# First projections of a two-layer trunk: plain fp32r products against seven block products in scaled fp16 parts

## The chip, the cores and the metric

The kernel runs on one core of a Trainium2 chip. The metric is the device time of one launch, in microseconds (us). The kernel before takes 2886.77 us, the median of three runs (2885.02 to 2900.39).

## The reference, cut to what matters

Two post-norm layers, `x <- LayerNorm(alpha * x + mixer(x))`, over 2048 tokens of 1024 features. Layer 0 is forgetting attention with 8 heads of 128, layer 1 sparse attention over keys chosen by an indexer. The change lies in the first statement of layer 0:

```python
def _fox_mixer(x, w_in, b_f, w_out):
    ...
    q, k, v, f_logit, gate = _split(x @ w_in, [H * dh, H * dh, H * dh, H, D])
    ...
    log_f = jax.nn.log_sigmoid((f_logit + b_f).astype(jnp.float32))
    cum = jnp.cumsum(log_f, axis=1)
    ...
    s = jnp.einsum('bqhd,bshd->bhqs', q_b, k).astype(jnp.float32) * scale
    s = s + jnp.transpose(c_b, (0, 2, 1))[..., None] - cum_t[:, :, None, :]
    ...
    return (jax.nn.silu(gate) * o.reshape(B, S, D)) @ w_out
```

`x @ w_in` is a product of 2048 x 1024 by 1024 x 4104: queries, keys and values of 1024 columns each, 8 columns of forget logits, and 1024 columns of gate.

## The kernel before, in words

The stages follow each other: the first projections (`fox_proj`), forgetting attention (`attention(0)`), its output projection with the projections and the index of layer 1, attention of layer 1, its output projection. TensorE goes through them without a break between stages.

**Precision.** A product of fp32 operands is made of three matmuls (`mm3`, lines 308 to 313): high part by high part (L310), high by low (L311), low by high (L312). In `fox_proj` the parts are of type fp32r. `split` (L318 to L320) makes them: ACT copies the high part (L319), and GpSimd (POOL) or, for tokens, VectorE (DVE) subtracts it for the low part (`sub`, L316).

**Tiles.** A query, key or gate tile is 128 columns of `w_in` (numbers 0 to 7 queries, 8 to 15 keys, 16 to 23 gates) by all tokens, in four chunks of 512 tokens. `weights` (L323) reads a tile as two pieces of 128 x 512 and splits each; `proj` (L331) makes 8 x 3 matmuls of 512 columns for a chunk into one bank of PSUM, weights stationary. That is 24 x 4 x 24 = 2304 matmuls. Values are turned: the tokens are stationary, the columns of the values move, in slices of 384, 384 and 264 columns (`VW`; the last has the 8 forget logits). `values` makes 16 x 24 matmuls for each slice: 768 of 384 columns, 384 of 264.

**Evacuation.** Gate tiles go through ACT (`to_dram`, L345). Queries, keys and values are scaled and cut into two fp16 parts for attention: ACT makes the high part (L352), DVE the rest (L353), and SP stores both.

**Scales and the scan.** The fp16 parts need scales, powers of two taken from the largest magnitudes of the tokens and of every weight tile. `bounds` (L455 to L532) is the scan: it reads the weights once more, 512 KB at a time through the two QS buffers (L477), DVE reduces each to a column of maxima (L470), `find` gathers them (L494), TensorE turns the columns (L496), DVE reduces across (L498), `spread` brings the results to all partitions with a small matmul (L502) and works out the scales (L503 to L523).

**Order.** The chunks of the first three gate tiles come first, while the tokens are loaded and split. The scan runs beside gate tiles 19 to 21, five reads a chunk (`SCAN`); `find` stands between the halves of tile 23. Then come the values' last slice, tile 0, the forget gates (`fox_gates`), and the rest. The order within an engine is set when the program is built: its scheduler places rows by the dependencies and by its own idea of time. SP issues all reads and stores in one order.

Of the kernel before, what the change touches and what calls it, by code (L numbers as in the profile page):

```python
# [41 lines left out]
VW = (384, 384, 264)  # L42
# [6 lines left out]
         {"K": 4, "V": 2, "PT": 1, "PU": 1, "PX": 1, "PR": 4, "PP": 3, "M": 1, "N": 3}, {"P": 8})  # L49
ORDER = ((), ("N", "I", "PR", "PT", "pad1", "PU", "K", "PP", "V", "PX"),  # L50
         ("N", "M", "PX", "PT", "PU", "pad2", "PR", "K", "V", "PP"), ("pad3", "P"))
SIZE = {"K": 2048, "V": 4096, "PT": 8192, "PU": 8192, "PX": 8192, "PR": 4096, "PP": 4096, "I": 128, "N": 256,
        "M": 2432, "pad1": 3200, "pad2": 896, "pad3": 4096, "P": 4096}
# [18 lines left out]
SCAN = 5  # L72
FINDS = (0, 1), (2, 3)
# [59 lines left out]
def lay_out(inp):  # L133
# [10 lines left out]
    o["fw"] = mtiles(np.concatenate([fw[:, 0:2048], fw[:, 3080:4104]], 1))  # L144
    for i, n in enumerate(VW):
        v = fw[:, 2048 + 384 * i:2048 + 384 * i + n].reshape(2, 4, 128, n)
        o["fv%d" % i] = c(v.transpose(0, 2, 1, 3).reshape(2, 128, 4 * n))
# [26 lines left out]
def trunk(tc, A, out, taps=None):  # L174
    nc = tc.nc
    with ExitStack() as ctx:
        K = Trunk(ctx, tc, A, out)
        with K.phase(0):
            K.fox_proj()
# [42 lines left out]
class Trunk:  # L222
    def __init__(self, ctx, tc, A, out):
# [28 lines left out]
        self.flog = self.sb.tile([128, NT, 8], F32, name="flog")  # L252
        self.wi = self.flog
# [4 lines left out]
    def constants(self):  # L258
        nc, A = self.nc, self.A
        mf = self.e([128, 128])  # L260
        nc.sync.dma_start(self.ident, A["ident"])
        nc.sync.dma_start(self.kvg, A["kvg"])
        nc.sync.dma_start(mf, A["cmask"])
        nc.sync.dma_start(self.zt, A["ztab"].rearrange("p (a b) -> p a b", a=4))
        nc.vector.tensor_copy(self.cmask, mf)
# [93 lines left out]
    def to_planes(self, name, row, scale):  # L359
        def evac(ps, ch):  # L360
            t, parts = self.pair()
            self.planes(parts, ps, scale)
            to = self.scr[name]
            to = to[ch, row:row + 128] if name == "q1" else to[row:row + 128, :, ch * 512:(ch + 1) * 512]
            self.nc.sync.dma_start(to, t)
        return evac

    def fox_proj(self):
        nc, A = self.nc, self.A
        X = {}  # L370
        xv = A["xT"].rearrange("(g k p) t -> g p k t", k=4, p=128)
        first = (16, 17, 18)
        W = {}
        for ch in range(NCH):
            for g in range(2):
                hi, lo = self.t("KV", [128, 4, 512], R), self.t("P", [128, 4, 512], R)
                for k in range(4):
                    if ch == 0 and (g, k) in ((0, 0), (0, 2), (1, 0)):
                        m = first[len(W)]
                        W[m] = self.weights(A["fw"][m])  # L380
                    raw = self.e([128, 512])
                    nc.sync.dma_start(raw, xv[g][:, k, ch * 512:(ch + 1) * 512])
                    self.split(hi[:, k], lo[:, k], raw, nc.vector)
                X[g, ch] = hi, lo
        self.constants()

        def tile(m, chunks=range(NCH)):
            row = m % 8 * 128
            evac = (self.to_planes("q1", row, self.scale("cq", 0)), self.to_planes("k1", row, self.scale("k", 0)),
                    self.to_dram("g1", row, AF.Silu))  # L390
            self.proj(W.get(m) or self.weights(A["fw"][m]), X, chunks, evac[m // 8])

        def values(s):
            n = VW[s]
            wv = []
            for g in range(2):
                hi = self.t("P", [128, 4, n], R)
                los = []
                for b in range(2):
                    raw = self.t("W", [128, 2, n])  # L400
                    nc.sync.dma_start(raw.rearrange("p k c -> p (k c)"), A["fv%d" % s][g][:, b * 2 * n:(b + 1) * 2 * n])
                    for k in range(2):
                        if g:
                            lo = self.e([128, n], R)
                        else:
                            if k == 0:
                                pair = self.t("QS", [128, 2, n], R)
                            lo = pair[:, k]
                        self.split(hi[:, 2 * b + k], lo, raw[:, k])
                        los.append(lo)  # L410
                wv.append((hi, los))
            heads = n // 128
            for i in range(NT):
                ps = self.acc()
                ch, o = i // 4, (i % 4) * 128
                for kt in range(8):
                    xh, xl = X[kt // 4, ch]
                    hi, los = wv[kt // 4]
                    self.mm3(ps[:, :n], xh[:, kt % 4, o:o + 128], xl[:, kt % 4, o:o + 128],
                             hi[:, kt % 4], los[kt % 4], kt == 0, kt == 7)  # L420
                ov = self.t("SC", [128, heads, 2, 128], F16)
                self.planes((ov[:, :, 0], ov[:, :, 1]), ps[:, :heads * 128].rearrange("p (h d) -> p h d", d=128),
                            self.scale("v", 0))
                nc.sync.dma_start(self.scr["v1"][3 * s:3 * s + heads, :, i].rearrange("h p a d -> p h a d"), ov)
                if s == 2:
                    nc.vector.tensor_copy(self.flog[:, i], ps[:, 256:264])

        for ch in range(NCH):
            for m in first:
                tile(m, (ch,))  # L430
        scan, find, spread = self.bounds(X)
        for m in (19, 20, 21):
            for ch in range(NCH):
                for job in islice(scan, SCAN):
                    job()
                tile(m, (ch,))
        for job in scan:
            job()
        W[22], W[23] = self.weights(A["fw"][22]), self.weights(A["fw"][23])
        tile(22)  # L440
        tile(23, FINDS[0])
        find()
        tile(23, FINDS[1])
        spread()
        values(2)
        tile(0)
        self.fox_gates()
        values(0)
        tile(1)
        tile(8)  # L450
        values(1)
        for m in (2, 3, 4, 5, 6, 7, 9, 10, 11, 12, 13, 14, 15):
            tile(m)
# [6 lines left out]
    def bounds(self, X):  # L460
# [4 lines left out]
        most = self.flog.rearrange("p a b -> p (a b)")  # L465
        used = [0]

        def largest(src):
            i, used[0] = used[0], used[0] + 1
            op = V.tensor_reduce(most[:, i:i + 1], src, axis=AX.XY if len(src.shape) > 2 else AX.X, op=OP.max,  # L470
                                 apply_absolute_value=True)
            self.follow(op, self.lead, "what the start needs comes first")

        def load(ap):
# [3 lines left out]
            largest(raw)  # L478

        fw, dw, uk = A["fw"], A["dw"], A["ukv"]  # L480
        groups = [[partial(largest, X[k][0].bitcast(F32).rearrange("p a b -> p (a b)")) for k in X]]
        groups += [[partial(load, fw[m]) for m in range(a, a + 8)] for a in (0, 8)]
        groups.append([partial(load, A["fv%d" % i][g][:, a:min(a + 1024, 4 * n)]) for i, n in enumerate(VW)
                       for g in range(2) for a in range(0, 4 * n, 1024)])
        groups += [[partial(load, dw[m]) for m in range(6, 14)], [partial(load, dw[0])]]
        groups += [[partial(load, uk[:, :768])], [partial(load, uk[:, 768:])], [partial(largest, self.kvg)]]
        groups += [[partial(load, A[n][0:1].rearrange("o (p c) -> (o p) c", p=128))] for n in ("lng", "lnb")]
        m = len(groups)
        col = self.t("mb", [128, m])
        b = self.t("mb", [128, m])  # L490

        def find():
            for i, a in enumerate(ends):
                V.tensor_reduce(col[:, i:i + 1], most[:, ends[i - 1] if i else 0:a], axis=AX.X, op=OP.max)  # L494
            self.tp = self.psum("T")
            turn = nc.tensor.transpose(self.tp[:m, :128], col, self.ident)  # L496
            self.follow(turn, self.lead, "no product waits for the bounds")
            V.tensor_reduce(col[:m, :1], self.tp[:m, :128], axis=AX.X, op=OP.max)  # L498

        def spread():  # L500
            tp = self.psum("T")
            nc.tensor.matmul(tp[:, :m], col[:m, :1].to_broadcast([m, 128]), self.ident[:m, :m], start=True, stop=True)  # L502
            V.tensor_copy(b, tp[:, :m])  # L503
            x, wq, wk, wv, wq2, wt, wuk, wuv, g, lg, lb = (b[:, i:i + 1] for i in range(m))
            z = self.scales
# [9 lines left out]
            z6 = z[:, :6]  # L515
            V.tensor_scalar(z6, z6, 1e-15, None, op0=OP.max)
            V.tensor_scalar(z6.bitcast(I32), z6.bitcast(I32), 0x7f800000, None, op0=OP.bitwise_and)
# [876 lines left out]
```

## Time and profile before

| what | value |
|---|---|
| median of three runs | 2886.77 us |
| profiled execution: its own time | 2880.37 us |
| profiled execution: span of its instructions | 2878.1 us |
| mean granted clock of TensorE | 0.974 |
| first matmul of the first projections | 6.99 us |
| first matmul of attention | 738.71 us |

PE is TensorE's matmul record, PEld its weight loads, DVE VectorE, ACT ScalarE, POOL GpSimd, SP the engine that issues most transfers. A row of the timeline has its start, its duration, engine, line, operation, the tile written and the tile read, and in brackets how long the engine had been idle and what released it. Matmuls overlap, so the distance between two starts, and not the duration, is what one costs. A row of groups has, after the bar, the busy time and the mean of one, then the idle time ahead of the group and what ended it.

### The profile page before, as it was taken

Reading aid. Unit: us, or ns where it says so; the run is one execution under the profiler, and the core shown is the slowest. Engines: PE = TensorE matmul, PEld = TensorE weight load, DVE = VectorE, ACT = ScalarE, POOL = GpSimd, SP = SyncE. Lnnn points to the kernel's source line nnn. Section 1 sums busy time; section 2 is a strip of 40 time slices with the busy share of each in tenths; the row PEclk is TensorE's granted clock in tenths of the full one; section 3 lists DMA queues with packets and bytes.
Section 4 is the critical chain, followed back from the end, with each engine's and each line's share of the span. In section 5 each row is a group of like instructions: output and inputs, shape, how many; then the busy total and the mean of one; then the engine's idle time right before and its main releaser. Section 6 shows DMA issues by size and latency. Waiting matters only on the chain. (4 is left out here: it accounts for less than half of the span.)

```text
span 2878.1 us, 41192 instructions
## 1 busy us (share of the span) xinstructions
PE 2668.3 (93%) x14608; PEld 2105.1 (73%) x14608; DVE 1690.9 (59%) x4311; ACT 1276.7 (44%) x2128; POOL 764.7 (27%) x520
## 2 busy tenths in 40 slices
PE   9999999999988888989999999999996998889898
PEld 7879998888666666768877778778773666666686
DVE  5332111111566666656627789988995666676565
ACT  4312211111566566631125685764734665666310
POOL 1411010110233334432222311223113343334421
PEclk9999999999999999999999999999997999999999
DMA  5852222222889877777366532445658888887642
GB/s 197 291 192 64 66 71 80 70 70 79 214 200 201 197 174 178 162 221 230 118 197 203 158 104 86 154 132 165 183 180 231 180 184 181 183 181 154 185 137 87
DMA packets 630213, 456.01 MB, mean 158 GB/s; under 512 B 386224, under 2 KB 499392, under 8 KB 630000
## 3 DMA queue, kind: packets, MB, share of 16 engines
q1 hardware_dynamic: 626960, 444.77, 57.2%
q10 hardware_dynamic: 1984, 4.20, 0.5%
q0 software_dynamic: 1056, 4.36, 0.4%
q8 instruction: 115, 1.88, 0.3%
q14 instruction: 98, 0.80, 0.1%
HBM read 237.71 MB, written 123.24 MB: 125 GB/s over the span
## 5 line engine op out<-in xcount | busy, mean ns | idle before, releaser
L316 POOL TENSOR_TENSOR W<-RW,W 128x512 fp32r<-128x512 f32 x240 | 317.6, 1340 | 1116.0 <-ACT W L319 1018.6
L316 POOL TENSOR_TENSOR PP<-PR,PP 128x640 f16<-128x640 f32 (+3 forms) x192 | 375.5, 1970 | 664.0 <-ACT PP L762 516.9
L754 ACT ACTIVATE PR<-PR,ty,scales 128x1152 f32<-128x1152 f32 (+15 forms) x256 | 330.1, 1290 | 255.4 <-DVE ty L753 255.1
L319 ACT ACTIVATE W<-RW 128x512 fp32r<-128x512 f32 x240 | 142.4, 628 | 382.1 <-PE O L311 129.5
L310 PE MATMUL T<-KV,W 128*128 128x512 f32 x688 | 274.3, 399 | 0.0
L312 PE MATMUL T<-KV,W 128*128 128x512 f32 x688 | 273.5, 398 | 0.0
L1205 DVE SCALAR_TENSOR_TENSOR P<-SC,flog,P 128x512 f32<-128x512 f32 (+2 forms) x266 | 193.4, 754 | 15.6 <-ACT SC L1200 14.3
L311 PEld LDWEIGHTS <-V 128*128 128x128 f16 x1152 | 117.3, 102 | 104.7 <-issue 81.5
L762 ACT ACTIVATE PP<-PR 128x640 f16<-128x640 f32 (+3 forms) x192 | 186.1, 980 | 6.8 <-DMA PU<-PP 1.8
L311 PE MATMUL U<-P,W 128*128 128x512 f32 x424 | 169.2, 399 | 1.9 <-DVE P L316 1.8
L311 PE MATMUL T<-KV,W 128*128 128x512 f32 x408 | 162.7, 399 | 0.0
L310 PE MATMUL O<-KV,W 128*128 128x512 f32 x392 | 157.2, 401 | 2.2 <-ACT E L345 2.2
L740 DVE CUSTOM_DVE_ANT_0 PR<-S,W,ty 128x512 f32<-128x512 f32 (+3 forms) x209 | 138.9, 664 | 34.4 <-PE S L735 14.0
L312 PE MATMUL O<-KV,W 128*128 128x512 f32 x392 | 157.0, 400 | 0.0
L310 PEld LDWEIGHTS <-V 128*128 128x128 f16 x1152 | 117.5, 102 | 53.3 <-DMA PX<-PP 9.5
L310 PEld LDWEIGHTS T<-KV,W 128*128 128x128 f32 x688 | 130.7, 190 | 30.8 <-issue 0.3
L312 PEld LDWEIGHTS T<-KV,W 128*128 128x128 f32 x688 | 130.5, 190 | 30.8
L310 PE MATMUL S<-K,E 128*128 128x512 f16 (+3 forms) x379 | 131.3, 347 | 11.8 <-DVE ty L740 11.3
L311 PE MATMUL O<-P,W 128*128 128x512 f32 x352 | 140.5, 399 | 1.6 <-DVE P L316 1.6
L311 PE MATMUL T<-P,W 128*128 128x512 f32 x344 | 137.1, 399 | 0.0
L312 PEld LDWEIGHTS <-V 128*128 128x128 f16 x1152 | 117.6, 102 | 19.9
L311 PE MATMUL S<-K,E 128*128 128x512 f16 (+3 forms) x379 | 131.5, 347 | 0.0
(393 smaller groups left out, 7088.3 us busy)
## 6 DMA issues: line engine op xcount, KB each, us to landing
RW<-in_dw SPq DMA_DIRECT2D x110, 256.0 KB
RW<-in_fw SPq DMA_DIRECT2D x66, 256.0 KB
scr_g<-E SPq DMA_DIRECT2D x64, 256.0 KB
E<-scr_g SPq DMA_DIRECT2D x64, 256.0 KB
scr_og<-SC SPq DMA_DIRECT2D x64, 256.0 KB
RW<-scr_og SPq DMA_DIRECT2D x64, 256.0 KB
E<-scr_q SPq DMA_DIRECT2D x62, 256.0 KB
scr_q<-E SPq DMA_DIRECT2D x56, 256.0 KB
```

The source lines that it names most:

```text
L310: first = mm(o, lh, rh, start=start, stop=False, skip_group_check=True)
L311: mm(o, lh, rl, start=False, stop=False, skip_group_check=True)
L312: mm(o, ll, rh, start=False, stop=stop, skip_group_check=True)
L316: eng.tensor_tensor(out=o, in0=a, in1=b, op=OP.subtract)
L319: self.nc.scalar.activation(hi, src, AF.Copy)
L740: nc.vector.tensor_tensor_reduce(out=row[:, lo:hi], in0=sc[:, lo - a:hi - a], in1=bias, op0=OP.add, op1=OP.min, scale=-1.0, scalar=3e38 if ...
L754: nc.scalar.activation(row, row, AF.Exp, bias=up, scale=neg, accum_out=cs["l"][:, j:j + 1])
L762: nc.scalar.activation(hi, row, AF.Copy)
L1205: nc.vector.scalar_tensor_tensor(x[:, a:b], t, w1, x[:, a:b], op0=OP.mult, op1=OP.add)
```

## The change

The first projections are made in another way.

- **Seven products.** Gate tiles 16 to 23 by chunks 0 and 1 stay plain fp32r products (384 matmuls). All the rest is cut into units: two weight tiles m and m+1 by a half of the tokens p (two chunks). A unit is a 2 x 2 block product, done by seven products of half the inner length (a form of Strassen's, in Winograd's arrangement) instead of eight. Each of the seven is four steps of the inner length by `mm3` in fp16 parts. Query, key and gate units (20) use 512 columns: 84 matmuls each. Value units (8, tokens stationary) use 128 columns (136 in the products that carry the forget logits): 336 matmuls each, and each has another stationary block.
- **Weights.** `fox_weights` reads a pair of tiles (128 x 2048), ACT scales it by a power of two (L403), POOL makes four sums or differences of blocks (L421, L316), and seven blocks are cut into fp16 parts: ACT (L319) and POOL (L316). Before, the two pieces of a tile were cut once, and the gate, query and key tiles served four chunks.
- **Tokens.** `fox_tokens` makes the seven blocks of each half: 28 steps of ACT (L466) and DVE (L467), with 16 differences on DVE. The tokens are read again for it (L449).
- **Evacuation.** `fox_unit` gathers four sums (a, b, c, d) in PSUM: two ACT copies (L507, L510), four DVE sums (L512, L514, L516, L523), one POOL sum (L517), and then what was there before.
- **The scan in two parts.** The blocks' scales need the maxima before the cuts. The early part (the second half's tokens, the value weights, the forget columns: 17 reads) runs beside the plain gate tiles, the late part (24 tiles of weights, 9 of layer 1, two of its smaller weights: 35 reads by QS) beside the fifth to the seventh value unit in the text of the program. `across` (L368 to L375) does the turning and spreading on TensorE and DVE, `power` (L381 to L383) the powers.
- **Order.** Plain gate tiles; four value units of the first half (V1 to V4), four of the second half (V5 to V8); four gate units of the second half; then queries and keys, both halves of a pair after each other.

The core of the diff:

```diff
+    def fox_weights(self, m):
...
+        nc.scalar.activation(flat, flat, AF.Copy, scale=s)
...
+        cut(0, a11)
+        cut(6, a22)
+        P.tensor_tensor(out=a22, in0=a21, in1=a22, op=OP.add)
+        cut(1, a22)
+        self.sub(P, a21, a11, a21)
+        cut(2, a21)
+        self.sub(P, a11, a22, a11)
+        self.sub(P, a22, a12, a11)
+        cut(3, a22)
+        cut(4, a11)
+        cut(5, a12)
...
+    def fox_unit(self, w, p, evac, tiles=None):
...
+            for a, j in enumerate(tiles or (0,)):
+                for k in range(4):
...
+                    if tiles:
+                        js, to = slice(j * 128, (j + 1) * 128), ps[:, a * wd:a * wd + more]
+                        op = self.mm3(to, xh[:, k, js], xl[:, k, js], wh[:, k, :more], wl[:, k, :more], start, stop)
+                    else:
+                        op = self.mm3(ps, wh[:, k], wl[:, k], xh[:, k], xl[:, k], start, stop)
...
-        scan, find, spread = self.bounds(X)
-        for m in (19, 20, 21):
-            for ch in range(NCH):
-                for job in islice(scan, SCAN):
-                    job()
-                tile(m, (ch,))
...
+        w = self.fox_weights(24)
...
+        order = [(m, 0) for m in (24, 26, 28, 30)] + [(m, 1) for m in (24, 26, 28, 30, 16, 18, 20, 22)]
+        order += [(m, None) for m in (0, 8, 2, 4, 6, 10, 12, 14)]
+        for n, (m, p) in enumerate(order):
...
+            if n + 1 < len(order):
+                later = self.fox_weights(order[n + 1][0])
+            if n < 4:
+                load1(n)
+            for i, _ in enumerate(unit(m, p or (p is None) * 1, w)):
+                if n < 4 and i < 7:
+                    make1(i, n)
+                if 4 <= n < 7:
+                    for job in islice(late, SCAN):
+                        job()
+            if n == 6:
...
+                find()
+                spread()
+                self.power(6, 12)
...
+            if n == 8:
+                self.fox_gates()
```

The instructions stand in other places on each engine. Three places matter below. The names are the program's tiles with their numbers: W and RW weights in parts, A raw blocks, X token parts, QS the buffers of the scan.

**First place: ACT around the first value unit.** Before, ACT alternates between cutting the weights of a tile (L319) and evacuating chunks (L345):

```order
L319 ACTIVATE W_119_774<-RW_121_776 128x512
L319 ACTIVATE W_119_774<-RW_122_780 128x512
L345 ACTIVATE E_94_656<-T_93_631 128x512
L319 ACTIVATE W_130_827<-RW_132_829 128x512
L319 ACTIVATE W_130_827<-RW_133_833 128x512
L345 ACTIVATE E_102_703<-U_101_678 128x512
```

After, the two scalings of the first two weight pairs, then a token cut (L466), and then the first cut of the first value unit's weights (L319 into W_125):

```order
L345 ACTIVATE E_115_827<-U_114_802 128x512
L403 ACTIVATE A_124_896<-A_124_896,powers_95 128x2048
L403 ACTIVATE A_140_946<-A_140_946,powers_95 128x2048
L466 ACTIVATE X_132_935<-A_145_972,powers_95 128x512
L319 ACTIVATE W_125_900<-A_124_896 128x4x128
L319 ACTIVATE RW_130_905<-A_124_896 128x512
L319 ACTIVATE RW_144_953<-A_140_946 128x512
```

The token cut of the second half stands ahead of the first weight cut, and evacuations of the plain gate tiles stand behind.

**Second place: the column of late maxima on TensorE, and what follows it on ACT and POOL.** Before, TensorE's transposing row stands among the plain products of gate tile 23, in its third chunk:

```order
L311 MATMUL O_223_1406<-P_39_201,W_206_1214 128x512
L312 MATMUL O_223_1406<-KV_38_200,W_207_1215 128x512
L310 MATMUL O_223_1406<-KV_38_200,W_206_1214 128x512
L496 MATMUL T_222_1403<-ident_84,mb_87_614 11x128
L311 MATMUL O_223_1406<-P_39_201,W_206_1214 128x512
L312 MATMUL O_223_1406<-KV_38_200,W_207_1215 128x512
L310 MATMUL O_223_1406<-KV_38_200,W_206_1214 128x512
```

After, the transposing row and the spreading row stand between the last product of V8 (into U_351) and the first product of the first gate unit (into S_365):

```order
L311 MATMUL U_351_4173<-RW_323_3608,X_138_941 128x128
L312 LDWEIGHTS X_138_941
L312 MATMUL U_351_4173<-RW_323_3608,X_138_941 128x128
L368 MATMUL O_339_4008<-ident_84,mb_337_3996 21x128
L373 MATMUL O_339_4008<-ident_84,ty_340_4010 128x21
L310 LDWEIGHTS W_342_4047
L310 MATMUL S_365_4466<-X_132_935,W_342_4047 128x512
L311 LDWEIGHTS W_342_4047
L311 MATMUL S_365_4466<-X_132_935,W_342_4047 128x512
```

ACT there, from the last evacuation of V8 to the first cut of that gate unit's weights (A_341 is its raw block, A_359 and A_386 those of the next two; L752 and L753 are the forget gates):

```order
L352 ACTIVATE SC_358_4434<-E_348_4120,tz_346_4069 128x4x128
L752 ACTIVATE QS_378_4579<-QS_378_4579 128x128
L753 ACT_TABLE_LOAD
L753 ACTIVATE QS_378_4579<-QS_378_4579 128x128
L403 ACTIVATE A_341_4043<-A_341_4043,powers_95 128x2048
L403 ACTIVATE A_359_4438<-A_359_4438,powers_95 128x2048
L403 ACTIVATE A_386_4647<-A_386_4647,powers_95 128x2048
L319 ACTIVATE W_342_4047<-A_341_4043 128x512
```

And POOL, from the last evacuation sums of the value units on:

```order
L517 TENSOR_TENSOR E_331_3878<-E_331_3878,E_328_3729 128x512
L517 TENSOR_TENSOR E_353_4320<-E_353_4320,E_350_4171 128x512
L316 TENSOR_TENSOR W_342_4047<-A_341_4043,W_342_4047 128x512
L316 TENSOR_TENSOR RW_345_4050<-A_341_4043,RW_345_4050 128x512
L316 TENSOR_TENSOR RW_363_4445<-A_359_4438,RW_363_4445 128x512
L316 TENSOR_TENSOR RW_390_4654<-A_386_4647,RW_390_4654 128x512
L421 TENSOR_TENSOR A_341_4043<-A_341_4043 128x512
L421 TENSOR_TENSOR A_359_4438<-A_359_4438 128x512
L421 TENSOR_TENSOR A_386_4647<-A_386_4647 128x512
L316 TENSOR_TENSOR A_341_4043<-A_341_4043 128x512
L316 TENSOR_TENSOR W_342_4047<-A_341_4043,W_342_4047 128x512
L316 TENSOR_TENSOR A_359_4438<-A_359_4438 128x512
```

What was one row among many products of TensorE now stands between two units, and POOL makes the blocks of three units by turns.

**Third place: the reads of the scan on SP.** Before, they stand between reads of weight pieces (L327) and stores of gate chunks (L346):

```order
L477 DMA QS_126_815<-in_fw 128x1024
L477 DMA QS_127_818<-in_fw 128x1024
L346 DMA scr_g1_72<-E_168_1021 128x512
L327 DMA RW_199_1172<-in_fw 128x512
L327 DMA RW_204_1206<-in_fw 128x512
L477 DMA QS_128_821<-in_fw 128x1024
L477 DMA QS_129_824<-in_fv0 128x1024
L346 DMA scr_g1_72<-E_179_1074 128x512
```

After, the first of the late reads (L667) stand behind the last store of V3 (SC_209) and a weight read into A_319, and between the stores of V4 (SC_228 to SC_231):

```order
L563 DMA scr_v1_65<-SC_209_2224 128x1024
L392 DMA A_319_3601<-in_fw 128x1024 x2
L667 DMA QS_241_2717<-in_fw 128x1024
L667 DMA QS_242_2720<-in_fw 128x1024
L563 DMA scr_v1_65<-SC_228_2539 128x1024
L563 DMA scr_v1_65<-SC_229_2594 128x1024
L667 DMA QS_245_2750<-in_fw 128x1024
L563 DMA scr_v1_65<-SC_230_2598 128x1024
L667 DMA QS_246_2753<-in_fw 128x1024
L563 DMA scr_v1_65<-SC_231_2653 128x1024
L667 DMA QS_248_2781<-in_fw 128x1024
```

The reads go through the same two QS buffers as before, now among the stores of the value units and the reads of weight pairs.

More of the change, by code (lines that the diff above doesn't have):

```diff
@@ new lines, in across @@
+    def across(self, cols, out, tag="O"):
+        nc, V = self.nc, self.nc.vector
+        n = cols.shape[-1]
+        ps = self.ps_tile(tag)
+        turn = nc.tensor.transpose(ps[:n, :128], cols, self.ident)
+        if self.lead:
+            self.follow(turn, self.lead, "no product waits for sizes")
+        top = self.tiny(1)
+        V.tensor_reduce(top[:n], ps[:n, :128], axis=AX.X, op=OP.max)
+        nc.tensor.matmul(ps[:, 128:128 + n], top[:n, :1].to_broadcast([n, 128]), self.ident[:n, :n],
+                         start=True, stop=True)
+        V.tensor_scalar(out, ps[:, 128:128 + n], 1e-15, None, op0=OP.max)
@@ L393, in values @@
[L393 to L426, printed above, removed]
@@ new lines, in fox_proj @@
+        early, late, find, spread = self.bounds()
+        rooms()
+        for n, m in enumerate((19, 20, 21, 22, 23)):
+            W[m] = self.weights(A["fw"][m])
+            if n < 4:
+                load(n)
+            for job in islice(early, 6):
+                job()
+            if n < 4:
+                for i in range(7):
+                    make(i, n)
+            if n == 4:
+                for job in early:
+                    job()
+            tile(m, (0, 1))
+        w = self.fox_weights(24)
@@ L458, in scale, with bounds, load @@
         return self.scales[:, i:i + 1]
-    def bounds(self, X):
+    def bounds(self):
         nc, A, V = self.nc, self.A, self.nc.vector
[L465 to L474, printed above, removed]
+        most, fw, dw, uk = self.most, A["fw"], A["dw"], A["ukv"]
+        xv = A["xT"].rearrange("(g k p) t -> g p k t", k=4, p=128)[:, :, :, 1024:]
+        def load(i, ap):
             n = ap.shape[-1]
@@ L485, in bounds @@
[L485 to L490, printed above, removed]
-        def find():
[L493 to L498, printed above, removed]
@@ L500, in spread, with row @@
-        def spread():
[L501 to L505, printed above, removed]
+            op = self.largest(most[:, i:i + 1], raw)
+            self.follow(op, self.lead, "what the start needs comes first")
+        def row(name):
+            return A[name][0:1].rearrange("o (p c) -> (o p) c", p=128)
```

303 lines of the change are left out of this document (235 added, 68 removed).

## The prediction

> **What bounds the kernel now.** I read the page's totals first, then windows by stage, the waits, and single rows of the timeline. The page's head, busy time by engine:
>
> ```profile
> span 2878.1 us, 41192 instructions
> PE 2668.3 (93%) x14608; PEld 2105.1 (73%) x14608; DVE 1690.9 (59%) x4311; ACT 1276.7 (44%) x2128; POOL 764.7 (27%) x520
> ```
>
> TensorE bounds it, and the stage of the change more than the rest. The windows view (PE, PEld, DVE, ACT, POOL busy, clock, DMA share, GB/s) over that stage:
>
> ```profile
> 7.00:170.00 163.00, 163.00 (x687) 130.92 (x688) 78.87 (x86) 56.01 (x96) 42.04 (x32) 1.00 0.74 246
> 170.00:195.00 25.00, 19.71 (x76) 15.42 (x75) 7.62 (x11) 4.18 (x9) 8.23 (x10) 0.86 0.57 192
> 195.00:736.00 541.00, 540.14 (x2694) 469.79 (x2693) 89.74 (x197) 94.31 (x161) 53.79 (x46) 1.00 0.23 73
> 500.00:600.00 100.00, 100.00 (x430) 80.59 (x429) 13.15 (x18) 16.55 (x26) 10.15 (x8) 1.00 0.20 69
> ```
>
> A 512-column fp32r matmul costs 100/430 = 0.233 us. 687 of them are 160.1 us, so the first window loses 2.9 us (the clock's start). The second loses 25 − 76×0.233 = 7.3 us, nearly all at one wait:
>
> ```profile
> PE T L496 <- DVE mb L494: 5.3, 1, 5.3
> ```
>
> That is the transpose of the column of maxima. TensorE's rows around it:
>
> ```profile
> 179.29 0.39 PE L310 MATMUL O<-KV,W 128*128 128x512 f32 x1
> 184.97 0.39 PE L496 MATMUL T<-ident,mb 128*11 128x128 f32 x1 [5.29 <-DVE mb L494]
> 186.01 0.63 PE L310 MATMUL O<-KV,W 128*128 128x512 f32 x1
> 186.43 0.63 PE L311 MATMUL O<-P,W 128*128 128x512 f32 x1
> ```
>
> After it, starts are 0.42 us apart instead of 0.23: half clock for a while, some 2 us lost per long wait. So the stage is matmul count times rate, plus waits for the scan of maxima.
>
> **The matmuls.** The last row of the stage and the rows of attention behind it give the fp16 prices; its last two are the ends of a run of 128-column products, and below are the weight loads that run ahead of them:
>
> ```profile
> 738.47 0.40 PE L312 MATMUL O<-KV,W 128*128 128x512 f32 x1
> 738.71 0.39 PE L310 MATMUL S<-QS,SC 128*128 128x512 f16 x1
> 740.01 0.22 PE L310 MATMUL U<-QS,SC 128*128 128x128 f16 x1
> 1019.91 0.22 PE L310 MATMUL O<-PX,V 128*128 128x128 f16 x1
> 1020.30 0.27 PE L310 MATMUL U<-K,E 128*128 128x256 f16 x1
> ```
>
> ```profile
> 1019.91 0.10 PEld L311 LDWEIGHTS <-V 128*128 128x128 f16 x1
> 1020.25 0.10 PEld L310 LDWEIGHTS <-E 128*128 128x128 f16 x1
> ```
>
> From 738.71 to 740.01 are six products of 512 columns: 0.216 us each. From 1019.91 to 1020.30 are seven of 128 columns: 0.056 each, with a weight load for every one, 0.056 apart as well. The stage after: 384 plain fp32r (gate tiles, chunks 0 and 1) × 0.233 = 89.5; twenty query, key and gate units of 7×4×3 = 84 × 0.216 = 362.9; eight value units of 336 × 0.056 = 150.5 (18.8 each), and about 1 for the 136-column ones. Sum 604 us, with the 2.9 of the start 607, from 7.0 to 614. Before, the stage runs from 7.0 to 738.7. With no waits the change would be worth 125 us; what it adds are waits.
>
> **Work of the other engines per unit.** The groups by shape, busy and mean ns of one:
>
> ```profile
> L316 POOL TENSOR_TENSOR W<-RW,W 128x512 fp32r<-128x512 f32 x66 | 85.1, 1304 | 420.6 <-ACT W L319 393.9 <-PE U L311 21.1 <-DMA RW<-in_fw 5.3
> L316 POOL TENSOR_TENSOR PP<-PR,PP 128x512 f16<-128x512 f32 x16 | 18.5, 1155 | 19.5 <-ACT PP L762 19.5
> L319 ACT ACTIVATE W<-RW 128x512 fp32r<-128x512 f32 x66 | 39.6, 627 | 126.1 <-PE O L311 67.8 <-DMA RW<-in_fw 26.1 <-PE T L311 13.9
> L762 ACT ACTIVATE PP<-PR 128x2048 f16<-128x2048 f32 x16 | 30.6, 1910 | 0.2
> L352 ACT ACTIVATE E<-U,scales 128x512 f16<-128x512 f32 x24 | 16.5, 689 | 106.8 <-PE U L312 106.8
> L353 DVE SCALAR_TENSOR_TENSOR E<-T,scales,E 128x512 f16<-128x512 f32 x24 | 18.0, 752 | 109.5 <-ACT E L352 109.5
> L316 DVE TENSOR_TENSOR P<-E,KV 128x512 fp32r<-128x512 f32 x32 | 24.1, 782 | 15.2 <-ACT KV L319 14.9
> L510 DVE TENSOR_TENSOR scales<-mb 128x1 f32<-128x1 f32 x6 | 0.6, 153 | 0.0
> L544 ACT ACT_TABLE_LOAD x1 | 1.3, 1283 | 0.0
> ```
>
> Weights of a unit: POOL 7 cuts × 1.155 + 4 sums × 1.30 = 13.3, with the sum of the evacuation 14.6 us. ACT: one scaling of 2048 columns 1.91 + 14 copies (7 of tokens) × 0.63 + 6 evacuations × 0.69 = 14.9. DVE: 7 × 0.78 + 4 × 0.78 for tokens, 8 × 0.75 for the evacuation = 14.6. All under 18.1 to 18.8 of TensorE: in steady units the cover holds by 4 us, and these cost nothing. They cost where TensorE has no work queued ahead, at two places.
>
> **Wait A, the first value unit.** TensorE's row for the early maxima stands after 336 plain matmuls, 7.0+2.9+78.3 = 88.2. The early scan is 17 reads, issued once the first three gate tiles have their two chunks (144 products, to 43.5 us); at 2.8 us each (below) it ends near 91: 2.4 us of wait. Behind it only 48 matmuls (11.2 us) hide the chain to the first cut weight: two scalings, 3.8 us, and then, in ACT's order above, a token cut ahead of the first weight cut. That one needs a read into a buffer that the first half's tokens hold: DVE has 44 token operations × 0.78 and 17 maxima × 1.22, 55 us from about 46 us on, so it is free near 101 and the read lands 2×2.8 − 1.2 = 4.4 later (an estimate throughout): first product near 108, plain work done at 102.6, so 5.7 us. POOL then makes the blocks of two units by turns: 7 more. A = 15 us; 8 if the read is early, 20 if all is late. Were the cover of 11 us gone too, A would be 26.
>
> **Wait B, the first gate unit after the eighth value unit.** It needs all late maxima: 35 reads of up to 512 KB through two buffers. What such reads cost before, the group by shape:
>
> ```profile
> L470 DVE TENSOR_REDUCE flog<-QS 128x1 f32<-128x1024 f32 x32 | 39.0, 1220 | 80.2 <-DMA QS<-in_fw 53.2 <-DMA QS<-in_dw 13.9 <-DMA QS<-in_fv 12.5
> ```
>
> and rows of DVE's timeline, to the reduction across at the end:
>
> ```profile
> 91.94 2.47 DVE L470 TENSOR_REDUCE flog<-QS 128x1 f32<-128x1024 f32 x2 [12.80 <-DMA QS<-in_fw]
> ...
> 155.77 1.22 DVE L470 TENSOR_REDUCE flog<-QS 128x1 f32<-128x1024 f32 x1 [1.17 <-DMA QS<-in_dw]
> ...
> 183.51 1.22 DVE L470 TENSOR_REDUCE flog<-QS 128x1 f32<-128x1024 f32 x1 [0.69 <-DMA QS<-in_ukv]
> 184.76 0.15 DVE L494 TENSOR_REDUCE mb<-flog 128x1 f32<-128x1 f32 x1
> 185.39 0.28 DVE L498 TENSOR_REDUCE mb<-T 11x1 f32<-11x128 f32 x1 [0.48 <-PE T L496]
> ```
>
> From 155.77 to 183.51 are 11 reads, 2.5 us each; from 91.94 to 183.51 are 30, 3.05 each. The DVE waits for the read each time. I take 2.8: 98 us. In SP's order the first late read stands behind a weight read (A_3601) that waits for POOL's last cut for V5, made during V4: some 12 us into V4, an estimate from POOL's 14.6. From there to the end of V8 TensorE has 5×18.8 − 12 = 82 us. So 16 us are exposed (5.5 at 2.5, 25 at 3.05). SP's stores of finished values queue between the reads, so a read never overtakes an evacuation; but no store is what TensorE waits for.
>
> Then the chain. Behind the waiting transpose TensorE has only that gate unit, and ACT, DVE and POOL only its weights and the forget gates, so nothing fills the time. From 184.76 to the end of L498 are 0.9 us, and the spread takes about as much again, 1.6 together; 18 small DVE operations × 0.155 = 2.8; on ACT the two functions and table load of the forget gates 1.9, and three scalings of 2048 columns 5.7, all ahead of the first cut; cut and difference 0.63 + 1.16. Sum 13.8 us. After it POOL's order (above) makes blocks of three units by turns: between the first and the second block of this unit stand 3 cuts, 4 sums and its own cut, 9.8 us against a product of 12 × 0.216 = 2.6, so 7.2; then 5.1 − 2.6 = 2.5; then 9.4 − 2.6 = 6.8. Sum 16.5. B = 16 + 13.8 + 16.5 = 46 us (36 to 55). The old wait, 5.3 us, is gone with L496.
>
> **Sum.** Half clock after the two waits, 2 us each: 4. At the end attention's first loads of values wait for the last stores in another order: 0 to 4, I take 2, since before the first attention product followed without a gap. 614 + 15 + 46 + 4 + 2 = 681 against 738.7: −58 us. Later stages keep their code but for one buffer's tag: nothing. On the profiled execution, 2880.4 (span and 2.3 around it), that is 2822.7; the median lies 6.4 above it, so 2829.
>
> **Rivals.**
>
> 1. Weight loads set the pace of the value units. They reuse each stationary token block for one 128-column product only, 336 in a row, and a weight load by itself is recorded at 102 ns:
>
> ```profile
> L311 PEld LDWEIGHTS <-V 128*128 128x128 f16 x1152 | 117.3, 102 | 104.7 <-issue 81.5
> ```
>
> If loads do not overlap in long runs, 2688 × 0.046 = +124 us; the longer units then hide the late scan (−16) and POOL's turns in A (−7), so −58 + 101 = +43: 2930. The rows at 1019.91 speak against it: loads start 0.056 apart while each is recorded as 0.10. But that run is seven long. It decides for slower from (58+23+14)/2688 = 0.035 over 0.056, 91 ns a product.
>
> 2. Half of that, loads hidden in part. At 80 ns: 2688 × 0.024 = +65, less the same 23, gives −16: 2871, at the edge of no change. The Trainium skill, "TensorE: Matmul & The Clock Gate", section Back-to-back issue gap, says that a stream of weight load and matmul pairs sustains about 81 ns at 128 columns; by that the sum would be −14. The same sentence gives 131 ns at 512 columns, where the trace has 216, so I hold it for less likely than the rows.
>
> 3. The waits are small: reads at 2.5 us, sums on POOL quicker than a cut, the token read early. A 8, B 20: −90, 2797.
>
> 4. The scan goes far slower beside the weights and stores (every 1 us a read is 35 us), or the sums starve several units. B 85 to 130: 2868 to 2913.
>
> 5. The seven products do not run at fp16's price. All rows say 0.216 against 0.233, and the count is in the order. At 0.233 it costs 29 us: 2858.
>
> **How the numbers follow.** This kernel's measurement can tell 0.5% (14 us) from no change. Forecast 0.54, its own range 2810 to 2846: the ends of A (−7, +5), of B (−10, +10) and 2 for the clock and the end. Rival 3: 0.10. Rival 5: 0.03. Rival 2: 0.13, half of it within 0.5%. Rival 1: 0.08. Rival 4: 0.12, by thirds faster, the same, slower. Faster 0.54+0.10+0.03+0.065+0.04 = 0.775, the same 0.065+0.04 = 0.105, slower 0.08+0.04 = 0.12. The range 2790 to 2880 leaves out rival 1, half of rival 4 and a little of rival 3, 0.16.
>
> **What the profile after would show.** The first attention product near 681 us. Value units of 18.8 us, their matmuls 0.056 apart: at 0.08 rival 2, at 0.1 rival 1. A group of waits of TensorE for the reduce of the late maxima of about 16 us with waits for the chain, ACT and POOL of some 30 behind it, and 15 near the first value unit. If the late reads come 3.5 us apart or more, rival 4. The forecast is wrong if steady gate units take over 18.5 us, since then POOL or ACT, not TensorE, sets their pace.

## The result, and the profile after

The changed kernel takes 2849 us in the median on record, against 2886.8: a ratio of 0.985, interval 0.981 to 0.989, some 43 us less where 58 were forecast. (The median counts one of four timed runs that was disturbed; the other three are 2841 to 2853 us with a median of 2844.9, and the ratio is made of those.) The profiled execution has a span of 2839.2 us, 38.9 less than before. The page's head, and its row of busy times:

```profile
span 2839.2 us, 44412 instructions
...
PE 2555.5 (90%) x15910; PEld 1893.8 (67%) x15910; DVE 1877.1 (66%) x4567; ACT 1417.3 (50%) x2318; POOL 997.0 (35%) x704
```

TensorE is busy 113 us less, 92 of it in the first projections; two thirds of the 113 come back as idle time of TensorE. Where: the windows view by stage, columns as before. The stretches are the plain gate tiles, the wait behind them, V1 to V4, V5 to V8, the first gate unit, and most of the rest of the first projections.

```profile
7.00:100.00 93.00, 87.06 (x364) 69.94 (x365) 75.67 (x118) 43.15 (x69) 20.45 (x15) 0.96 0.77 266
100.00:127.00 27.00, 15.84 (x141) 13.87 (x140) 14.98 (x20) 16.68 (x29) 18.49 (x15) 0.81 0.36 112
115.25:222.60 107.35, 85.38 (x1344) 84.73 (x1344) 80.41 (x86) 59.98 (x102) 83.77 (x68) 0.86 0.37 123
222.60:326.00 103.40, 82.44 (x1348) 81.29 (x1344) 67.24 (x90) 27.96 (x49) 40.13 (x35) 0.92 0.75 242
343.60:372.00 28.40, 24.50 (x87) 9.61 (x88) 6.29 (x20) 10.30 (x19) 28.30 (x25) 0.77 0.10 34
390.00:700.00 310.00, 309.95 (x1437) 140.40 (x1436) 105.48 (x147) 113.03 (x173) 138.73 (x113) 1.00 0.27 94
```

The last row is as forecast: 1437 products in 310 us, 0.216 each, TensorE never idle. The third and the fourth are not: four value units of 336 products take 107 and 103 us where 75 were forecast. TensorE's waits over the stage, from the waits view (total, times, longest):

```profile
PE U L310 <- DVE E L514: 20.0, 3, 7.9
PE T L310 <- DVE E L514: 14.4, 3, 7.5
...
PE O L368 <- DVE mb L716: 6.2, 1, 6.2
```

The wait for the late maxima, the last row, is 6.2 us, not 16. The largest item is one that the forecast has no term for: L514, a sum in the evacuation, 35 us in all, 19.6 of it in V1 to V4 and 15.5 in V5 to V8. TensorE's timeline at such a wait, and at the end of V8:

```profile
141.12 0.22 PE L312 MATMUL S<-W,X 128*128 128x128 f16 x1
141.68 0.22 PE L310 MATMUL T<-W,X 128*128 128x128 f16 x1
149.35 0.26 PE L310 MATMUL T<-RW,X 128*128 128x128 f16 x1 [7.45 <-DVE E L514]
149.41 0.31 PE L311 MATMUL T<-RW,X 128*128 128x128 f16 x1
149.51 0.31 PE L312 MATMUL T<-RW,X 128*128 128x128 f16 x1
...
325.70 0.22 PE L312 MATMUL U<-RW,X 128*128 128x128 f16 x1
332.10 0.40 PE L368 MATMUL O<-ident,mb 128*21 128x128 f32 x1 [6.18 <-DVE mb L716]
...
343.60 0.61 PE L310 MATMUL S<-X,W 128*128 128x512 f16 x1 [10.12 <-ACT W L319]
```

From 141.12 to 141.68 are ten products, 0.056 each: long runs of 128-column products with a new weight load each do keep their price, so rivals 1 and 2 are out. The Trainium skill, "TensorE: Matmul & The Clock Gate", section Back-to-back issue gap, has 81 ns for such a stream; the rows here say 56. After the wait of 7.45 us starts are 0.10 apart (149.41 to 149.51): half clock, which costs V1 to V8 another 14 us or so.

Why L514? The text of `fox_unit` says it. The seven products go into the sums `SUMS = "acdcbad"`: the third and the seventh share bank d. Behind the fifth, DVE makes u from b (L512) and z from what d holds then (L514), and only then may the seventh add to d. TensorE has little ahead to fill that time: the sixth product, 2.7 us (1.35 in V1 and V5, which are made in two halves; the rows above are of the second half of V1), and what the scheduler drew forward of the next unit. DVE's timeline over the same time:

```profile
140.40 1.31 DVE L467 SCALAR_TENSOR_TENSOR X<-A,powers,X 128x512 f16<-128x512 f32 x1
141.64 1.75 DVE L316 TENSOR_TENSOR A<-A 128x512 f32<-128x512 f32 x1
143.31 1.64 DVE L467 SCALAR_TENSOR_TENSOR X<-A,powers,X 128x512 f16<-128x512 f32 x1
144.87 0.41 DVE L512 TENSOR_TENSOR E<-U,E 128x256 f32<-128x256 f32 x1
145.20 1.04 DVE L353 SCALAR_TENSOR_TENSOR SC<-E,tz,SC 128x256 f16<-128x256 f32 x1
146.16 1.75 DVE L316 TENSOR_TENSOR A<-A 128x512 f32<-128x512 f32 x1
...
148.22 0.74 DVE L467 SCALAR_TENSOR_TENSOR X<-A,powers,X 128x512 f16<-128x512 f32 x1
148.88 0.41 DVE L514 TENSOR_TENSOR E<-T,E 128x256 f32<-128x256 f32 x1
```

Four operations stand between L512 and L514 (one is left out here). L512 itself is late: the fifth product's last matmul starts at 137.02, and DVE reaches L512 at 144.87, behind a row of token operations and evacuations, the last three of which are shown. And they are long: L316 of this shape takes 1.75 here. The groups of DVE by shape, 100 to 330 us:

```profile
L361 DVE TENSOR_REDUCE ztab<-QS 128x1 f32<-128x1024 f32 x33 | 40.2, 1218 | 36.0 <-DMA QS<-in_fw 25.7 <-DMA QS<-in_dw 10.1
L467 DVE SCALAR_TENSOR_TENSOR X<-A,powers,X 128x512 f16<-128x512 f32 x29 | 32.9, 1149 | 13.0 <-ACT X L466 13.0
L316 DVE TENSOR_TENSOR A<-A 128x512 f32<-128x512 f32 x16 | 22.8, 1426 | 0.2
L353 DVE SCALAR_TENSOR_TENSOR SC<-E,tz,SC 128x512 f16<-128x512 f32 x18 | 18.7, 1040 | 5.4 <-ACT SC L352 5.4
L353 DVE SCALAR_TENSOR_TENSOR SC<-S,tz,SC 128x512 f16<-128x512 f32 x4 | 3.0, 739 | 0.0
```

What reads two operands from SBUF is long (1.15, 1.43, 1.04 us, in place of 0.74, 0.68, 0.75 alone); the last row, the same operation with one operand from PSUM (S), is not, nor is the reduction with one operand.

### The profile page after: what moved, and what is told of

Its sections match the earlier page's. It is cut to its first block, busy times and chain, and to the rows that moved or that the text cites. A ratio compares the mean times of both kernels' runs of the same rounds, so it can differ in the third digit from the quotient of the medians.

```text
span 2839.2 us, 44412 instructions
## 1 busy us (share of the span) xinstructions
PE 2555.5 (90%) x15910; PEld 1893.8 (67%) x15910; DVE 1877.1 (66%) x4567; ACT 1417.3 (50%) x2318; POOL 997.0 (35%) x704
## 5 line engine op out<-in xcount | busy, mean ns | idle before, releaser
L316 POOL TENSOR_TENSOR PP<-PR,PP 128x640 f16<-128x640 f32 (+3 forms) x192 | 375.7, 1971 | 606.4 <-ACT PP L971 459.5
L316 POOL TENSOR_TENSOR W<-RW,W 128x512 fp32r<-128x512 f32 x190 | 253.4, 1351 | 729.0 <-ACT W L319 612.7
L319 ACT ACTIVATE W<-RW 128x512 fp32r<-128x512 f32 x190 | 112.6, 628 | 269.0 <-PE U L311 90.3
L316 POOL TENSOR_TENSOR W<-A,W 128x512 f16<-128x512 f32 x120 | 146.7, 1239 | 149.4 <-ACT W L319 149.4
L310 PE MATMUL T<-KV,W 128*128 128x512 f32 x400 | 156.9, 392 | 1.9 <-DVE sv L1542 1.8
L311 PE MATMUL T<-KV,W 128*128 128x512 f32 x400 | 156.3, 391 | 0.0
L312 PE MATMUL T<-KV,W 128*128 128x512 f32 x400 | 156.2, 390 | 0.0
L352 ACT ACTIVATE SC<-E,tz 128x512 f16<-128x512 f32 (+1 forms) x78 | 53.4, 685 | 197.3 <-DVE E L516 128.8
L310 PE MATMUL S<-K,E 128*128 128x512 f16 (+3 forms) x379 | 131.9, 348 | 12.4 <-DVE ty L949 11.7
L311 PE MATMUL S<-K,E 128*128 128x512 f16 (+3 forms) x379 | 131.6, 347 | 0.0
L312 PE MATMUL S<-K,E 128*128 128x512 f16 (+3 forms) x379 | 131.4, 347 | 0.0
L1409 ACT ACTIVATE SC<-S 128x512 f32<-128x512 f32 (+2 forms) x182 | 98.2, 548 | 50.5 <-DVE P L1414 28.7
L1483 ACT ACTIVATE P<-P,sv 128x1024 bf16<-128x1024 f32 (+6 forms) x88 | 103.1, 1171 | 36.5 <-DVE sv L1523 25.4
L311 PEld LDWEIGHTS <-X 128*128 128x128 f16 x896 | 92.2, 103 | 41.7 <-issue 41.7
L983 PE MATMUL T<-ident,PR 128*128 128x128 f32 x768 | 117.5, 278 | 2.7 <-DVE PU L316 1.7
```

The costliest lines, as they stand in the source:

```text
L310: first = mm(o, lh, rh, start=start, stop=False, skip_group_check=True)
L311: mm(o, lh, rl, start=False, stop=False, skip_group_check=True)
L312: mm(o, ll, rh, start=False, stop=stop, skip_group_check=True)
L316: eng.tensor_tensor(out=o, in0=a, in1=b, op=OP.subtract)
L319: self.nc.scalar.activation(hi, src, AF.Copy)
L983: nc.tensor.transpose(ps[:, (k - a) * 128:(k - a + 1) * 128], row[:, k * 128:(k + 1) * 128], self.ident)
```

## The experiments

The first theory after the result, P: an operation of DVE with two SBUF operands and one of POOL shut each other out, so DVE reaches L514 late. Its rival, W: DVE simply has too much in a fixed order. A second question came from the later stages, which the change does not touch: they are 18 us shorter, and their fp32r products start closer together (rows below).

**e1, the kernel before again, and e2, the changed kernel again**, with traces from one chip.

> The kernel before, unchanged, with a trace of its own on the chip of the next three runs. In the stages that the change does not touch, plain fp32r products of 512 columns start 0.233 us apart in the trace of before and 0.227 in the trace of after; some 4,400 of them lie there, 28 us. If that belongs to the chip or the hour, this trace shows 0.227 here and a time near 2850 us; if it belongs to the kernel, 0.233 and 2880 to 2890 us.

> The changed kernel, unchanged. If the 0.227 us belongs to the kernel, its later fp32r products start 0.227 us apart again, and it takes 2840 to 2855 us with the kernel before at 2885 on the same chip; if it belongs to the chip, both kernels have the same distance here and the ratio is 0.99 to 1.0. The value units again take some 210 us in all, with waits for L514.

e1: 2886 us, products 0.233 apart. e2: 2844 us, ratio 0.9864 (0.984 to 0.989), 0.227 apart. The distance belongs to the program. V1 to V4 take 108.3 us in e2.

**e3, token operations with one SBUF operand.**

```diff
+        self.zero = self.ps_tile("O")[:, :1]
+        V.memset(self.zero, 0.0)
+        self.zero = self.zero.to_broadcast([128, 512])
...
-                self.sub(V, b11, b12, b11)
+                self.sub(V, b11, b12, zero if p else b11)
...
-            V.scalar_tensor_tensor(lo, src, s, hi, op0=OP.mult, op1=OP.subtract)
+            V.scalar_tensor_tensor(lo, hi if p else src, 1.0 if p else s, zero if p else hi, op0=OP.mult, op1=OP.subtract)
```

> Each of the 44 token operations of DVE in the first four value units (28 low parts, 16 differences) reads one operand from SBUF and a zero from PSUM in place of its second SBUF operand, so the low parts of the second half's tokens are not the true ones; counts, shapes and what each waits for stay. Theory of the port (an operation of DVE with two SBUF operands and one of POOL hold each other up, DVE falls behind, TensorE waits for banks): these operations take 0.70 to 0.78 us also beside POOL, in place of up to 1.79, and value units 1 to 4 take 85 us or less in place of 107. Rival (DVE and ACT have too much to do in a fixed order, or reads come late): units 1 to 4 stay within 102 to 112 us.

The groups of DVE, 100 to 330 us, and the window of its V1 to V4:

```profile
L468 DVE SCALAR_TENSOR_TENSOR X<-X,O 128x512 f16<-128x512 f16 x28 | 18.5, 681 | 17.1 <-ACT X L467 17.1
...
L316 DVE TENSOR_TENSOR A<-A,O 128x512 f32<-128x512 f32 x16 | 10.8, 678 | 0.0
```

```profile
111.98:201.11 89.13, 81.56 (x1345) 81.02 (x1345) 59.22 (x91) 60.52 (x103) 73.46 (x68) 0.93 0.41 133
```

681 and 678 ns beside the same POOL work (the low parts, L468, now also read fp16 in place of fp32; the differences, L316, keep their type and are as short); DVE is busy 59 us instead of 80, V1 to V4 take 89 us instead of 107, and the kernel 2824 us. Four us more than P allowed, far below what W did: the same number of operations, in much the same order, cost 18 us of stage time by where one operand lies. What is left there, 6.8 us of waits for the same sum among it, was not traced to its cause. The Trainium skill, "SBUF — State Buffer", section SBUF: two separate sides, states just this: VectorE with two SBUF inputs and GpSimd take turns at one shared pair of ports for whole instructions. The trace agrees, with 1426 ns against 678.

**e4, the four sums of weight blocks on DVE instead of POOL.**

```diff
-        P.tensor_tensor(out=a22, in0=a21, in1=a22, op=OP.add)
+        V.tensor_tensor(out=a22, in0=a21, in1=a22, op=OP.add)
...
-        self.sub(P, a21, a11, a21)
+        self.sub(V, a21, a11, a21)
```

> The four sums and differences of weight blocks move from POOL (1.3 us each and more) to DVE (0.68 by itself) in every unit. Theory of the port: POOL holds the port 5.2 us less in a unit and DVE 2.8 more, so value units 1 to 4 take 5 to 15 us less in all, the time falls by 5 to 20 us against the changed kernel; gate, query and key units stay at 18.13 us. Rival (too much work on DVE): 2.8 us more of DVE's work in each of units 1 to 4 makes them 8 to 12 us longer, and units 5 to 7, with the maxima, too.

2830 us, ratio 0.981 (0.979 to 0.983), 14 us below e2. Its V1 to V4:

```profile
113.69:214.00 100.31, 81.92 (x1344) 80.54 (x1344) 85.40 (x106) 60.09 (x101) 59.10 (x47) 0.93 0.39 130
```

DVE is busy more, yet the units are 8 us shorter, and POOL is busy 24 us less. That is against W, and as P had it. V5 to V8 gain nothing (105.0 us, 102.5 in e2). The first gate unit takes 22.0 us instead of 27.1, but the second 21.3 instead of 18.5; V1 begins 3.5 us earlier (the two traces of the changed kernel differ by 1.9 there). Together the first projections end 11.6 us earlier than in e2.

**e7, the eighth PSUM bank in the rotation, and e8, that with e4.**

```diff
-FTAGS = "STUSTUS"
+FTAGS = "STUSTUSO"
```

> The changed kernel with the eighth PSUM bank in the rotation of the units' sums, so that a unit takes all four banks from the unit before the last one instead of one from the unit just ahead. If TensorE waits in the value units because the bank of that unit is freed late (L514 late on DVE), the 35 us of waits for L514 go, with some 10 of half clock; the late scan then ends later than the units, so that of 45 some 15 to 28 us are left as a gain: 2818 to 2832 us. If the value units are held by the supply of weights or tokens, the waits move to the cuts and the time stays within 5 us of the changed kernel's.

> Both: the eighth bank, and the four sums of weight blocks on DVE. By the theory of the port and of the bank the gains partly add: 2808 to 2825 us. If the sums on DVE only helped by freeing the bank earlier, this equals the run with the eighth bank within 5 us.

e7: 2846 us; e8: 2832 us, as e2 and e4. The forecast of a gain was wrong. V1 to V4 take 108.1 us in e7, the waits for L514 stay (15.6 and 13.9 us in its two largest rows). The bank that TensorE waits for is not one of the unit before: it is bank d of the same unit, and no rotation frees it. That is how I came to read `SUMS` as told above. No run gave the seventh product a bank of its own, so this link stands on the program's text and the rows. (In e7 the end of V8 is no test: its sum in the eighth bank comes behind the turning of the late maxima, which uses that bank too, and TensorE waits 17.2 us there.) e8 was forecast at 2808 to 2825 us and missed as well.

**e5, the kernel before with all pools moved by 32 bytes, and e6, the changed kernel moved by 32.** The changed kernel's new tile of 160 bytes lies ahead of all pools, and moves them; this was the first guess at the 0.227.

```diff
+        self.nc.vector.memset(self.sb.tile([128, 8], F32, name="gap"), 0.0)
```

> The kernel before with one unused tile of 32 bytes a partition (and its memset) ahead of the large pools, which moves all of them from addresses of remainder 32 to remainder 0 by 64; nothing else differs. Theory of the address: the changed kernel's 160-byte tile of powers had moved them so, and that is what makes fp32r products 0.227 us instead of 0.233. Then this kernel's 6520 products of 512 columns start 0.227 apart, some 42 us are saved, with the 384-column ones up to 46: 2838 to 2845 us, as fast as the changed kernel. Rival (the cadence comes with the changed program, by its instructions or their number): 0.233 and 2880 to 2888 us.

> The changed kernel with the same unused 32 bytes, which moves its large pools to remainder 32, where those of the kernel before lie. Theory of the address: its 4600 fp32r products of 512 columns cost 0.233 again, 29 us: 2870 to 2878 us, a gain of the change by itself of 5 to 15 us. Rival (the program): 0.227 and 2840 to 2850 us.

Both expectations fell: e5 keeps 0.233 and e6 keeps 0.227 (2851 us, 0.9888). But e5 is 27 us faster than the kernel before (2855.6 us, 0.990, interval 0.988 to 0.993) with nothing moved but addresses, which neither theory had said.

**e9, e10, e11, the distance.** What differs between the two kernels and not within these pairs is the distance from the staging pools (weight tiles W) to the stage pools (moving operands): 63168 bytes before, 63232 after.

```diff
-BUFS = {"W": 6, "E": 8, "RW": 3, "QS": 2, "SC": 3, "ty": 9, "tz": 4, "tb": 2, "mb": 2}
+BUFS = {"W": 6, "E": 8, "RW": 3, "QS": 2, "SC": 3, "ty": 9, "tz": 4, "tb": 4, "mb": 2}
```

> The kernel before with two more small tb tiles (64 bytes), which lie between the staging pools (W, E, QS) and the large pools of the stages (KV, P), so that the distance from a weight tile to its moving operand goes from 63168 to 63232 bytes, a multiple of 128 as in the changed kernel; the order of all engines is unchanged. If that distance sets the cadence of the fp32r products, they start 0.227 us apart, some 42 us less: about 2840 us. If not, 0.233.

> The kernel before with the 160 bytes of the changed kernel's powers as an unused tile ahead, and the 64 bytes of the run before it: W, RW, E and every pool of the later stages lie at exactly the addresses that they have in the changed kernel, and the order of all engines is that of the kernel before. If addresses set the cadence, 0.227 us in the later stages, 27 us there and 42 in all: 2838 to 2845 us. If the cadence comes with the changed program in some other way, 0.233, and a time between 2850 (as the kernel moved by 32 bytes) and 2885 us.

> The changed kernel with the same two more tb tiles: the distance goes from a multiple of 128 to 64 beyond one. If the distance sets the cadence: 0.233 us, 29 us more, 2870 to 2878 us. If not: 0.227 and 2840 to 2855 us.

The last stage is the same code in all. Its products in the timeline, first the kernel before, then e9, then e11:

```profile
2729.99 0.40 PE L310 MATMUL S<-P,W 128*128 128x512 f32 x1
...
2731.39 0.40 PE L310 MATMUL S<-P,W 128*128 128x512 f32 x1
```

```profile
2730.05 0.39 PE L311 MATMUL S<-P,W 128*128 128x512 f32 x1
...
2731.41 0.39 PE L311 MATMUL S<-P,W 128*128 128x512 f32 x1
```

```profile
2729.79 0.39 PE L312 MATMUL S<-P,W 128*128 128x512 f32 x1
...
2731.39 0.39 PE L310 MATMUL U<-P,W 128*128 128x512 f32 x1
```

Six steps in 1.40 us, 0.233; six in 1.36, 0.227; seven in 1.60, 0.229. So the distance sets it, and no instruction of e9 changed place. Neither pool's own place does: e9 has its staging pools where the kernel before has them, and the stage pools start at a multiple of 256 both in e5 (0.233) and in e12 below (0.227). e9 takes 2863 us in its one execution, where about 2840 were expected. The kernel before at the changed kernel's addresses (e10, 0.227) takes 2858 us, ratio 0.991 (0.988 to 0.994): 24 us gained by unused bytes. The expectation of 42 was too high: its first stage gives 13.7 (attention begins at 725.0 instead of 738.71), as 2304 × 0.0066 = 15 say, but the later stages wait for other things and give about 11 of their 28. e11 was to be slower, at 0.233, and is faster, 2826 us, 0.980 (0.978 to 0.982), with products 0.229 to 0.231 apart. It gained as e5 did, and in both the stage pools start at a multiple of 256 bytes.

**e12, e4 with 64 bytes ahead**, which keeps the distance and puts the stage pools at 81664, a multiple of 256.

```diff
+        self.nc.vector.memset(self.sb.tile([128, 16], F32, name="gap"), 0.0)
```

> The changed kernel with the sums of weight blocks on DVE, and an unused tile of 64 bytes ahead of all pools: the distance from weight tiles to moving operands stays 63232 (0.227 us a product, as in the run without the tile), and the large pools of the stages come to lie at multiples of 128, as they did in the two runs (the kernel before moved by 32 bytes, the changed kernel with the 64-byte gap) in which TensorE waited 34 us instead of 47 for the turned parts of P in the second attention. If that address is the cause, the waits are 34 us here too and the time falls by 8 to 15 us against the run with the sums on DVE alone (2829.9), to 2815 to 2822. If those two runs had it from elsewhere, 47 us and 2825 to 2836.

2797.9 us, ratio 0.971 (0.969 to 0.973): the fastest of all, 32 us below e4, where 8 to 15 were expected. TensorE's largest waits for the turned parts of P (transposing DMAs) in the second attention, in e4 and then in e12:

```profile
PE O L310 <- DMA PT<-PP: 20.2, 7, 5.3
PE O L310 <- DMA PX<-PP: 10.3, 6, 2.9
PE O L310 <- DMA PU<-PP: 9.9, 5, 2.7
PE U L310 <- DMA PX<-PP: 5.8, 3, 4.5
```

```profile
PE O L311 <- DMA PT<-PP: 13.2, 5, 3.5
PE O L311 <- DMA PX<-PP: 7.7, 5, 2.4
PE O L311 <- DMA PU<-PP: 6.9, 6, 2.0
PE U L311 <- DMA PX<-PP: 4.6, 2, 4.1
```

46.2 us against 32.4. With all such rows added, the three traces whose stage pools start at a multiple of 256 (e5, e11, e12) have 33 to 34 us, the other eleven 43 to 50: that the address is the cause is shown. The windows of the second attention, e4 and then e12:

```profile
2105.90:2645.40 539.50, 449.89 (x3196) 321.38 (x3194) 341.53 (x1028) 317.67 (x470) 193.75 (x102) 0.91 0.80 178
2096.60:2606.60 510.00, 436.33 (x3197) 314.93 (x3195) 341.84 (x1028) 317.49 (x470) 193.94 (x102) 0.95 0.78 189
```

This stage alone is 29.5 us shorter (the two profiled executions differ by 38.7). TensorE is idle 16 us less in it, nearly all in these waits, and is busy 13.6 us less with the same products, at a granted clock of 0.95 in place of 0.91. The pairs of e5 and e11 show the same stage 17 and 16 us shorter. What else went, some 9 us, was not traced.

## Why the prediction came out as it did

The sign and the range held; the sum did not hold by its own steps. The value units took 52 us more than forecast, the wait behind them and the later stages some 20 and 18 less. That these nearly met was luck.

| term, us | forecast | measured |
|---|---|---|
| end of the plain gate tiles | 102.6 | 107.1 |
| wait up to the first value unit | 5.7 | 8.2 |
| V1 to V8, with POOL's turns | 158.5 | 210.5 |
| end of V8 to the first gate unit | 29.8 | 17.9 |
| first gate unit, its products | 18.1 | 18.1 |
| POOL's turns in it, half clock | 18.5 | 10.2 |
| the other 19 units | 344 | 346 |
| half clock after the first wait, passage to attention | 4 | in the other rows |
| end of the first projections | 681 | 718 |
| later stages | 0 | −18 |

(The forecast's 102.6 is 0.8 more than its own terms, 88.2 + 2.4 + 11.2. The measured 718 has attention's first nine products in it, 1.5 us.)

**The matmul sum was right**: 0.056, 0.216 and the counts hold. The plain products cost 0.227, not 0.233: 2 us.

**The step that failed: "in steady units the cover holds by 4 us, and these cost nothing."** For the query, key and gate units it held (310 us without idle time); for the value units it did not: V1 to V8 took 210.5 us, not 158.5. The step compared totals of engines over a unit (14.6 of 18.8) and took durations from rows of work done alone or nearly so. Two things were wrong with it. POOL and DVE were added up each by itself; with the shared ports, V1 to V4 hold them for 14.6 us of POOL and some 11 of DVE (4 differences, 7 low parts, 3 or 4 evacuations) in a unit of 18.8, more than it has (an estimate from the forecast's own durations; the four units took 26.8 us each). e3 and e4 bear it out. The row L316 DVE of the forecast carried the sign of it, a mean of 0.78 us where the plain time is 0.68. And a total is the wrong measure where a chain inside a unit has a cover of 2.7 us and little more: product five, L512, L514, product seven. In V5 to V8 there are no token operations, and the same link still breaks, on the reads of the scan. The changed kernel's DVE in V6:

```profile
264.94 0.68 DVE L512 TENSOR_TENSOR E<-U,E 128x512 f32<-128x512 f32 x1
269.77 1.22 DVE L361 TENSOR_REDUCE ztab<-QS 128x1 f32<-128x1024 f32 x1 [4.15 <-DMA QS<-in_fw]
270.91 0.68 DVE L514 TENSOR_TENSOR E<-T,E 128x512 f32<-128x512 f32 x1
```

DVE stands 4.15 us at a maximum whose read has not landed, with L514 behind it, and TensorE's seventh product starts at 271.64. The forecast asked who waits behind SP's stores; it should have asked it of DVE's queue. V5 to V8 lost 28 of the 60 us that V1 to V8 took over their 150.5 us of products, 15.5 of them in waits for L514. This part was read from rows, and no run tried it. e4 takes POOL's sums off the ports there too, and V5 to V8 take 105.0 us, 102.5 in e2, which speaks against the ports as their cause.

**Wait A** had the right size by the wrong link. The token read was there in time: ACT began the two scalings at 102.75 only, behind four evacuations of plain tiles, and they took 3.92:

```profile
102.27 0.62 ACT L345 ACTIVATE E<-U 128x512 f32<-128x512 f32 x1
102.75 3.92 ACT L403 ACTIVATE A<-A,powers 128x2048 f32<-128x2048 f32 x2
...
107.37 0.61 ACT L319 ACTIVATE W<-A 128x512 f16<-128x512 f32 x1
```

**Wait B**: 28 us, not 46 or 48. The chain from the maxima to the first product was priced well, 11.5 us (332.10 to 343.60) against 13.8. The scan itself was slower than forecast, 3.1 us a read instead of 2.8, and took 114 us from the issue of its first read (217.84) to its last maximum (332.04); it was hidden to all but 6 us because the value units beside it, priced at 82 us, lasted 108. POOL's turns and the half clock cost less, 10.2 us. A term that rests on a cover moves with the cover.

**"Later stages: nothing"** was wrong, by 18 us in the profiled executions, and this is what brought the total near the forecast. At equal addresses the change alone is worth 2858 to 2844, 14 us (0.9864/0.9911 = 0.995, with some 0.4% either way): in the trace the first projections end at 718.35 instead of 725.0, and the later stages are 7 us shorter too, for which no cause is shown. Of the 43 us measured some 24 would have come from unused bytes alone (e10). Rival 4 had the mechanism, starved units, but put the price on the scan.

## What to carry to other kernels

Look for the chain inside a unit, and hold it against the work that really lies between its ends; totals of engines per unit say nothing about it. Where VectorE's operations with two SBUF operands run beside GpSimd's, add their times as if they were one engine. Before a gain of one per cent is put down to an edit, run the old kernel at the new kernel's addresses: a small new tile moves everything behind it.

## What the runs showed of the hardware

- The distance between the SBUF addresses of weights and moving operand sets the pace of fp32r products of 512 columns: 0.2267 us at 63232 bytes (247 × 256), 0.2333 at 63168, 0.229 to 0.231 at 63296. The fp16 products keep 0.216. The Trainium skill, "SBUF — State Buffer", section SBUF: two separate sides, has TensorE's ports wait for nobody; in these runs its own pace goes with where its two operands lie to each other, by what mechanism is not shown.
- Stage pools at a multiple of 256 bytes shorten TensorE's waits for transposing DMAs (46 to 32 us in the second attention from e4 to e12). The Trainium skill, "DMA: Bandwidth & Descriptors", section How a descriptor splits into AXI transactions, has transfers split at 256-byte boundaries, which fits; three placements at such a multiple were faster, and none at an odd multiple of 128 was tried, so 256 rather than 128 is only likely.
- A VectorE operation of 0.68 us with two SBUF operands took up to 1.77 beside GpSimd; with one operand in PSUM 0.68.
